# Another order of seven down-projection products, loads spread over items, and pinned weight sums in the up projection

## The chip, the cores and the metric

The kernel runs on one core of one Trainium2 chip. The metric is the device time of one execution in microseconds; the median over several runs is compared. A core has TensorE (PE) for matmuls, VectorE (DVE) and ScalarE (ACT) for elementwise work, GpSimd (POOL) and SyncE (SP), the last two here mostly issuing DMA transfers. Each engine works through its own queue in order; semaphores make one wait for another.

## The reference

One inference step of a two-layer encoder. There are 1024 frames of a prompt and 8 x 16 frames of running streams, T = 1152 tokens of width 1024. Layer 0 mixes with stick-breaking attention beside a convolution module, layer 1 with chunk-band attention; each layer ends with a squared-ReLU MLP of width 4096:

```python
def sq_relu_mlp(h, w_up, w_down):
    return jnp.square(jax.nn.relu(h @ w_up)) @ w_down

for layer in range(DEPTH):
    ...
    xp = xp + op
    xs = xs + os_
    xp = xp + sq_relu_mlp(rmsnorm(xp, norm_ffn[layer]), w_up[layer], w_down[layer])
    xs = xs + sq_relu_mlp(rmsnorm(xs, norm_ffn[layer]), w_up[layer], w_down[layer])
y_prompt = rmsnorm(xp, norm_final)
y_sample = rmsnorm(xs, norm_final)
```

All is float32. Beside y the step returns the new keys, values and convolution states. The change lies in the MLPs and at their borders.

## The kernel before, in words

**Data.** Activations lie feature by token, in tiles of 128 features by 1152 tokens. A product keeps float32 accuracy by splitting each operand into a high and a low part: ACT copies the high part (L180), DVE subtracts it to get the low part (L181), and each product is three matmuls (high by high and two mixed ones, `SPLIT`). One matmul has 288 token columns, a quarter of the tokens (TQ); TW = 576 is half of them.

**The MLP** of a layer is the function `rest`. It first finishes the out projection (evictions `evac`, L1303) and makes sums of activations (`combine`). Then both matrix products of the MLP are done by Strassen and Winograd's scheme, a 2x2 block product in seven products instead of eight.

*Up projection*: 16 units (`unit(m)`), each with products k = 0 to 6 of 24 matmuls. `seven(i)` makes the split weight of product i = 7m + k out of two raw tiles of `w_up` (`raw`, L1318 to L1323): for k = 1 the sums s1 = a21 + a22 (L1336), a21 - a11 (L1337) and s1 - a11 (L1338), the last being the weight of product 1; s1 itself is that of product 2; for k = 4 there is a difference at L1345. Split weights rotate through four tiles of a ring ("hl_m") and two others ("hl0", "hl1", printed as hl00 and hl10). The products go through three PSUM banks per token quarter. `take` evicts them: product 0 is copied by ACT (L1415), products 1 and 2 are added to the copy (L1417, L1419), and the quarters of the hidden block are finished at L1423 (product 4), L1426 (product 5) and L1429 (product 6). `done` then scales by the norm (L1394), applies relu and square on ACT (L1395, L1396), and makes three sums of the hidden blocks for the down projection, t3, t2 and b12 (L1400 to L1402); a fourth is `last_sum` (L1365). The seven combinations of hidden blocks go to DRAM (hb_d) through POOL's queue.

*Down projection*: seven products of 16 items each, 112 items, 24 matmuls per item (L1576). `todos` lists them in the order of `chains`; products of one chain accumulate in the same eight PSUM banks. Before, the chains are (3), (0, 1, 4), (2, 5), (6), and in layer 1 the last product is done one token quarter after another, with items of 12 matmuls. The loop at the end of `rest` does for each item i: load the hidden block and weight of item i + 4 (`load`), split those of i + 2 (`prep`: `split_b` for the hidden block, `split_w` for the weight), and the matmuls (`item`). At the last item of a product DVE adds the banks to the residual (L1582). Weight blocks a11, a21 and a22 are loaded once and stay (`resident`); products 3, 5 and 6 stream theirs. When a quarter of the output (a feature half by a token half) is final, `then` hands out the squares and splits of the next norm, done a step at a time among the later items. At item 104 of layer 0 `soon` loads and splits the first two weight chunks (each in two halves of 256 KB) of layer 1's first projection, through the staging tiles "st" that the streamed weights use.

**What sets the order.** The instructions are recorded in program order and then a list scheduler orders each engine's queue by its own estimates. `tc.keep_in_program_order` (`pinned`) keeps an instruction behind everything recorded before it on its engine. In the down projection nearly all of DVE's and ACT's work is pinned; in `seven` nothing is. DMA issues of loads stand in SP's queue in order.

Of the kernel before, what the change touches and what calls it, by code (L numbers as in the profile page):

```python
# [78 lines left out]
def level(steps, extra):  # L79


    pe, dve = sum(s.pe for s in steps), sum(s.dve for s in steps + extra)
    out, at, done, extra = [], 0.0, 0.0, list(extra)
    for s in steps:
        while extra and done + 0.5 * extra[0].dve < at / pe * dve:
            done += extra[0].dve
# [4 lines left out]
    return out + extra

# [27 lines left out]
def tile_trunk(ctx, tc, ins, outs):  # L120
# [1091 lines left out]
    def rest(layer, ks, cat, rst, mp, then, soon=None):  # L1212
# [112 lines left out]
        def seven(i):  # L1325
# [8 lines left out]
            elif k == 1:  # L1334
                s1 = ups["s1"] = sp.tile([P, 512], F32, "st", f"s1{name}{m}")
                tt(s1, a21, a22, ALU.add)  # L1336
# [16 lines left out]
            split(w[:, 0], w[:, 1], src)  # L1353
# [7 lines left out]
        pinned = tc.keep_in_program_order  # L1361
# [117 lines left out]
        def halves_of(t):  # L1479
            return [t[:, :512], t[:, 512:1024]]  # L1480

        def resident(kind, j):

            to = {"a11": a11, "a21": a21, "a22": a22}[kind]
            if j % 2 == 0:
                if kind == "a22":
                    tag = ("sl8", "sl9", "sl10", "sl11", "lo0", "lo1", "lo2", "xr3")[j // 2]
                    t = own(tag, F32)
                else:
                    t = place(j // 2, 0 if kind == "a11" else 1, F32, f"w{name}")  # L1490
                to[j], to[j + 1] = halves_of(t)
# [3 lines left out]
        def load(i):  # L1495

            if i >= len(todos):
                return
            k, ns, j = todos[i]
            if i == 0:  # L1500
# [6 lines left out]
            if k in (3, 5) or k == 6 and ns[0] == 0:  # L1507
                streams[i] = staging(wd[2 * j + 1][:, 512:] if k == 6 else wd[2 * j + 1][:, :512], f"wd{layer}{i}")
# [9 lines left out]
        def split_w(i):  # L1518
            k, ns, j = todos[i]
            if ns == (1,):  # L1520
                ws[i] = ws[i - 16]
                return
            if k == 3 or k == 6:
                src = streams.pop(i)
            elif k == 5:
                src = streams.pop(i)
                pinned(tt(src, src, a22[j], ALU.subtract))
# [6 lines left out]
            else:  # L1534
                src = a11[j] if k == 0 else a21[j]
            if k == 6 and layer == 1:
                w = pair(place(j // 2, j % 2, F32R, f"wk{name}"))
            elif k == 6:
                if j < 8:
                    tag = ("sl8", "sl9", "sl10", "sl11", "lo0", "lo1", "lo2", "xr3")[j]  # L1540
                    asplit.append(pair(own(tag, F32R)))
                w = asplit[j % 8]
# [7 lines left out]
        def prep(i):  # L1550
            if i < len(todos):
                split_b(i)
                split_w(i)

        def begin(n):

            if n == 0:
                for i in range(4):
                    load(i)
            else:  # L1560
                prep(0)
                prep(1)
# [3 lines left out]
        def item(i):  # L1566
            k, ns, j = todos[i]
            first = any(k == chain[0] for chain in chains) and j == 0
            b, w = bs.pop(i), ws[i]
            for m in range(4):  # L1570
                for n in ns:
                    if first:
                        banks[m, n] = bank(f"pd{layer}{k}{m}{n}")
                    ps = banks[m, n][:, :TQ]
                    for s, (a, h) in enumerate(SPLIT):
                        mm(ps, w[:, a, m * P:m * P + P], b[:, h, (n - ns[0]) * TQ:(n - ns[0]) * TQ + TQ],  # L1576
                           start=first and s == 0, stop=j == NF // 2 - 1 and s == 2,
                           skip_group_check=not any(k == chain[0] for chain in chains))
                    if j == NF // 2 - 1:
# [3 lines left out]
            if j == NF // 2 - 1 and k in final:  # L1583
# [11 lines left out]
        sq = Turns([extra[:, :TW], extra[:, TW:]])  # L1595
        for i in range(len(todos)):
            if i == 3:
                last_sum(NF // 2 - 1)
            if 2 <= i < 18:
                resident("a11", i - 2)  # L1600
            if 14 <= i < 30:
                resident("a21", i - 14)
            if 16 <= i < 32:
                resident("a22", i - 16)
            c = {n: m for m, n in enumerate((6, 7, 8, 9, 40, 41, 42, 43))}.get(i)
            if c is not None:
                x[c] = own(f"sl{c}", F32)
                dma(x[c], xr_d[layer][c])
            load(i + 4)
            prep(i + 2)  # L1610
            if 18 <= i < 34:
                pinned(tt(a21[i - 18], a21[i - 18], a11[i - 18], ALU.subtract))
# [6 lines left out]
        for go in later:  # L1619
# [219 lines left out]
```

## Time and profile before

| | us |
|---|---|
| runs | 2825.31, 2830.28, 2831.74 |
| median | 2830.28 |
| profiled execution | 2830.25 |
| its span | 2828.5 |
| out projection's end and unit 0, layer 0 (644 to 668) | 24.0 |
| up, layer 0 (668 to 1022.6) / layer 1 (2095 to 2447) | 354.6 / 352.0 |
| down, layer 0 (1022.6 to 1392) / layer 1 (2447 to 2816) | 369.4 / 369.0 |
| TensorE busy | 2705.3 |

A row of the timeline has the start in us, the time of the group, engine, line, operation, output tile <- input tiles, shape, the count, and in brackets the idle time before it and what ended it. A row of waits has who waited <- for whom, us in total, how many times, the longest. DVE at a line of the helper `split` has L181, ACT L180; the tile's name says which split it is.

### The profile page before, as it was taken

The page shows a single profiled execution, that of the slowest core. Times are in us where ns is not written, and L with a number is a line of the kernel's source. Part 1 is how long each engine was busy: PE and PEld are TensorE (multiplying, and loading weights), DVE is VectorE, ACT ScalarE, POOL GpSimd, SP SyncE. Part 2 cuts the span into 40 slices and gives each one's busy share as a digit, 9 for nine tenths or more (in the row PEclk, how much of TensorE's full clock was granted, in tenths as well). Part 3 has the DMA queues.
Part 4 walks back from the last instruction along what each step waited for, and adds up shares of the span by engine and source line. Part 5 has one row for each costly group of instructions (what it writes and reads, how often), then busy time and mean ns, then how long its engine had stood idle before and what let it go on. Part 6 is the DMA issues. An engine that isn't in the chain of part 4 may idle for free.

```text
span 2828.5 us, 50713 instructions
## 1 busy us (share of the span) xinstructions
PE 2705.3 (96%) x19362; PEld 2592.1 (92%) x19362; DVE 2146.1 (76%) x4201; ACT 1380.5 (49%) x2898; POOL 329.5 (12%) x599
## 2 busy tenths in 40 slices
PE   8988988899999999999999999998999999999998
PEld 8987876799999999999899999997999999999998
DVE  8999999978777756667467777778787777657676
ACT  5344446665444444445355555555554444434344
POOL 1000101032111110000011111110221111100001
PEclk9999998999999999999999999999999999999999
DMA  4434346443433486336444444446533334873355
GB/s 155 129 98 132 107 138 191 155 163 132 136 134 133 148 302 230 102 96 201 144 143 135 137 136 136 136 131 216 185 131 138 133 134 144 287 252 93 93 147 163
DMA packets 177811, 431.29 MB, mean 152 GB/s; under 512 B 26480, under 2 KB 54320, under 8 KB 175520
## 3 DMA queue, kind: packets, MB, share of 16 engines
q1 hardware_dynamic: 140304, 296.77, 33.6%
q0 software_dynamic: 37120, 131.27, 13.6%
q8 instruction: 152, 2.49, 0.4%
q14 instruction: 91, 0.75, 0.1%
q10 hardware_dynamic: 144, 0.02, 0.0%
HBM read 297.98 MB, written 117.34 MB: 147 GB/s over the span
## 4 chain that ended last, share of the span: by engine, by line
PE 51%; DVE 24%; DMA 10%; ACT 8%; issue 6%; SPq 0%; POOL 0%; DVEq 0%; ACTq 0%; POOLq 0%
PE pd L1576 19%; PE psc L220 10%; PE um L1388 9%; DMA xr<-in_w_up_dram 4%; DVE y L669 4%; DMA st_wd<-in_w_down_dram 3%; DVE kp L843 3%; PE avc L401 2%; DVE hl_m L181 2%; PE tpc L389 2%; DVE sg L845 1%; PE psoa L220 1%; PE f L220 1%; DMA wm<-in_w_down_dram 1%; DVE wla L181 1%
## 5 line engine op out<-in xcount | busy, mean ns | idle before, releaser
L220 PE MATMUL psc<-h,hl_wc 128*128 128x384 f32 x1728 | 327.2, 340 | 0.0
L220 PEld LDWEIGHTS psc<-h,hl_wc 128*128 128x128 f32 x1728 | 296.8, 188 | 13.3 <-issue 10.9
L1388 PE MATMUL um<-sl,hl_m 128*128 128x288 f32 x1548 | 244.1, 299 | 8.3 <-DVE hdm L1423 8.3
L1388 PEld LDWEIGHTS um<-sl,hl_m 128*128 128x128 f32 x1548 | 220.1, 191 | 10.7 <-ACT hdm L1396 5.8
L1576 PE MATMUL pd<-tm,hl_wd 128*128 128x288 f32 x1536 | 211.0, 296 | 2.1 <-DVE hl_wd L181 0.8
L1576 PEld LDWEIGHTS pd<-tm,hl_wd 128*128 128x128 f32 x1536 | 205.3, 189 | 4.5 <-DVE hl_wd L181 1.9
L669 DVE SCALAR_TENSOR_TENSOR y<-u,dw,y 128x1024 f32<-128x1024 f32 (+1 forms) x232 | 176.5, 809 | 0.4
L220 PE MATMUL psp<-h,hl_wi 128*128 128x384 f32 x864 | 169.0, 345 | 0.2 <-ACT kps L892 0.2
L1395 ACT ACTIVATE hdm<-hdm 128x288 f32<-128x288 f32 x192 | 84.4, 439 | 165.2 <-DVE hdm L1394 165.2
L220 PEld LDWEIGHTS psp<-h,hl_wi 128*128 128x128 f32 x864 | 149.7, 190 | 6.4 <-issue 4.9
L181 DVE TENSOR_TENSOR tm<-xr,tm 128x576 fp32r<-128x576 f32 (+1 forms) x120 | 85.7, 715 | 76.4 <-ACT tm L180 76.4
L180 ACT ACTIVATE tm<-xr 128x576 fp32r<-128x576 f32 (+1 forms) x120 | 77.8, 648 | 97.1 <-PE pd L1576 68.0
L1388 PE MATMUL um<-sl,hl 128*128 128x288 f32 x756 | 120.2, 297 | 4.4 <-DVE hdm L1423 4.4
L1104 ACT ACTIVATE s<-s,mxc 128x640 f32<-128x640 f32 (+4 forms) x128 | 88.8, 694 | 60.2 <-DVE mxc L1101 58.6
L180 ACT ACTIVATE hl_m<-xr 128x512 fp32r<-128x512 f32 x132 | 80.7, 621 | 71.8 <-DVE xr L1338 56.0
L1388 PEld LDWEIGHTS um<-sl,hl 128*128 128x128 f32 x756 | 106.5, 188 | 6.6 <-DVE hdm L1423 5.8
L1576 PE MATMUL pd<-th,hl_wd 128*128 128x288 f32 x768 | 108.3, 296 | 2.5 <-DVE th L181 2.3
L1576 PE MATMUL pd<-xr,hl_wd 128*128 128x288 f32 x768 | 108.1, 296 | 0.4 <-DVE hl_wd L181 0.4
L1576 PEld LDWEIGHTS pd<-th,hl_wd 128*128 128x128 f32 x768 | 103.7, 189 | 3.5 <-DVE th L181 3.0
L1576 PE MATMUL pd<-tm,hl 128*128 128x288 f32 x768 | 105.1, 295 | 0.0
L1576 PEld LDWEIGHTS pd<-xr,hl_wd 128*128 128x128 f32 x768 | 103.7, 189 | 1.2 <-DVE hl_wd L181 0.8
L181 DVE TENSOR_TENSOR hl_m<-xr,hl_m 128x512 fp32r<-128x512 f32 x132 | 92.3, 700 | 16.2 <-ACT hl_m L180 15.1
(527 smaller groups left out, 6814.4 us busy)
## 6 DMA issues: line engine op xcount, KB each, us to landing
xr<-hb_d SPq DMA_DIRECT2D x208, 288.0 KB, 2.9
xr<-in_w_up_dram SPq DMA_DIRECT2D x64, 512.0 KB, 4.8
hb_d<-hdm POOLq DMA_DIRECT2D x96, 288.0 KB, 3.7
hb_d<-t POOLq DMA_DIRECT2D x96, 288.0 KB, 3.7
st_wd<-in_w_down_dram SPq DMA_DIRECT2D x96, 256.0 KB, 3.4
wm<-in_w_down_dram SPq DMA_DIRECT2D x64, 256.0 KB, 6.0
st_wc<-in_w_in_c_dram SPq DMA_DIRECT2D x48, 256.0 KB, 2.8
xm_d<-xo POOLq DMA_DIRECT2D x16, 576.0 KB, 3.5
```

The costliest lines, as they stand in the source:

```text
L180: ACT(hi, src, AF.Copy)
L181: return tt(lo, src, f(hi), ALU.subtract)
L220: mm(ps()[:, :G], hl[:, a, at:at + P], act[g][k // 4][b][:, k % 4, :], start=n == 0, stop=n == len(todo) - 1)
L389: nc.tensor.transpose(tp[:, c0 + q * P:c0 + (q + 1) * P], blocks.get(j, tile_q), ident)
L401: mm(st["av"][:, o0:o0 + n], vs[:, j, i].rearrange("p a d -> p (a d)"), src[:, c0:c0 + n], start=st["done"] == 0, stop=st["done"] == nmm - 1)
L669: stt(src if j == CW - 1 else dst, src, wj, dst, ALU.mult, ALU.add)
L843: nc.vector.tensor_tensor_scan(keep[:, 0:n][:, ::-1], keep[:, 0:n][:, ::-1], ones[:, 0:1].to_broadcast([P, n]), 1.0, ALU.mult, ALU.mult)
L845: tt(w[:, 0:n - 1], w[:, 0:n - 1], keep[:, 1:n], ALU.mult)
L1104: ACT(s[:, :n], s[:, :n], AF.Exp, bias=mx, scale=-1.0, accum_out=tot)
L1388: mm(banks[b, n][:, :TQ], w[:, a, c * P:c * P + P], combo(key, c)[:, h, n * TQ:n * TQ + TQ], start=k < 3 and c == 0 and i == 0, stop=c == ...
L1395: ACT(y, y, AF.Relu)
L1576: mm(ps, w[:, a, m * P:m * P + P], b[:, h, (n - ns[0]) * TQ:(n - ns[0]) * TQ + TQ], start=first and s == 0, stop=j == NF // 2 - 1 and s == ...
```

## The change

1. *Up projection.* The sum s1 is pinned. So are the splits of product 0's weight, from unit 1 on. s1 of unit m + 1 is recorded in unit m just before product 6, behind the eviction of product 5 with its sums L1400 to L1402.

2. *Down projection.* The chains are (6), (3), (0, 1, 4), (2, 5), in layer 1 (6), (3), (0, 1, 4), (2), (5), where product 2 adds to two output quarters and product 5 goes quarter by quarter. The first half of the tokens is final after product 4, the fifth of seven, where before its last part came with the seventh product. Product 6 uses the resident a22, so 32 streamed 256-KB loads fall away. Item 0 opens all eight banks at once. Loads and splits are listed per item in a table `ahead_of`: a11 at items 8 to 23, a21 at 28 to 43, the residual at 2, 4, 6, 8 and 24 to 27; in layer 1 half of the last product's weights are split during product 2.

3. *First loads of layer 1.* `soon` now returns twelve steps, done at items 100 to 111 of layer 0: each of the four loads goes into half of the tile t1 and is split two items later.

4. At the borders the token order is mirrored: layer 1's first projections take token thirds 0, 1, 2 instead of 2, 0, 1, and the output's tail is the last 288 tokens instead of the second quarter.

The core of the diff:

```diff
+        pinned = tc.keep_in_program_order
...
                 s1 = ups["s1"] = sp.tile([P, 512], F32, "st", f"s1{name}{m}")
-                tt(s1, a21, a22, ALU.add)
+                pinned(tt(s1, a21, a22, ALU.add))
                 tt(a21, a21, a11, ALU.subtract)
                 tt(a11, s1, a11, ALU.subtract)
...
-            split(w[:, 0], w[:, 1], src)
+            if k == 0 and m:
+                pinned(ACT(w[:, 0], src, AF.Copy))
+                pinned(tt(w[:, 1], src, f(w[:, 0]), ALU.subtract))
+            else:
+                split(w[:, 0], w[:, 1], src)
...
-        chains = ((3,), (0, 1, 4), (2, 5), (6,))
-        out = {3: [(0, 0)], 0: [(0, 0)], 1: [(0, 1)], 4: [(1, 0), (1, 1)], 2: [(1, 1)], 5: [(0, 1)], 6: [(1, 0)]}
-        final = {0: (0, 0), 2: (1, 1), 5: (0, 1), 6: (1, 0)}
+        chains = ((6,), (3,), (0, 1, 4), (2, 5))
+        out = {6: [(1, 0)], 3: [(0, 0)], 0: [(0, 0)], 1: [(0, 1)], 4: [(1, 0), (1, 1)], 2: [(1, 1)], 5: [(0, 1)]}
+        final = {0: (0, 0), 4: (1, 0), 2: (1, 1), 5: (0, 1)}
...
+            chains = (*chains[:-1], (2,), (5,))
+            out[2].append((0, 1))
+            todos[6 * NJ:] = [(5, (n,), j) for n in range(2) for j in range(NJ)]
...
+        for i, (k, ns, j) in enumerate(todos):
+            at(max(-2, i - 4), load_b, i)
+            when = i - 2
+            if layer == 1 and k == 5:
+                when = 5 * NJ + 2 * j if j < 8 else i - 1 - (NJ - 1 - j)
+            at(max(-2, when - 2), load_w, i)
+            at(max(-1, i - 2), split_b, i)
+            at(max(-1, when), split_w, i)
...
+        for n, go in enumerate(soon(extra[:, TW:TW + 512]) if soon else []):
+            at(100 + n, go)
...
-            if i == 104 and soon:
-                soon()
```

Three places show how instructions move. The first is DVE in layer 0's up projection. The names: um0610 is the bank of layer 0, unit 6, bank 1, quarter 0; s1m06 the sum s1 of unit 6; hl_m043 the weight of its product 1 (43 = 7 x 6 + 1). Before, s1m06 stands among the evictions of unit 4:

```order
L1338 TENSOR_TENSOR xr20_6077<-s1m05_7990,xr20_6077 128x512
L1419 TENSOR_TENSOR tm00_6082<-um0420_7853,tm00_6082 128x288
L1336 TENSOR_TENSOR s1m06_8237<-xr10_6076 128x512
L1337 TENSOR_TENSOR xr10_6076<-xr10_6076,xr00_6075 128x512
L1419 TENSOR_TENSOR tm10_6083<-um0421_7867,tm00_6082 128x288
L181 TENSOR_TENSOR hl_m036_7994<-xr20_6077,hl_m036_7994 128x512
L1394 TENSOR_TENSOR th0_6723<-um0400_7788,rm0_6818 128x288
L1394 TENSOR_TENSOR th0_6723<-um0401_7802,rm0_6818 128x288
L181 TENSOR_TENSOR hl_m037_8032<-s1m05_7990,hl_m037_8032 128x512
L1423 TENSOR_TENSOR hdm0_51_6724<-um0410_7821,tm00_6082 128x288
```

In the changed kernel (line numbers are 5 to 9 higher: L1409 to L1411 are L1400 to L1402, L1438 is L1429, L1403 is L1394) the end of unit 5 and the making of unit 6's weights read so:

```order
L1409 TENSOR_TENSOR t10_6087<-hdm0_60_6725,hdm0_61_6726 128x576
L1403 TENSOR_TENSOR hdm0_61_6726<-hdm0_61_6726,rm0_6818 128x288
L1410 TENSOR_TENSOR t10_6087<-hdm0_60_6725,t10_6087 128x576
L1411 TENSOR_TENSOR hdm0_60_6725<-hdm0_60_6725 128x576
L1342 TENSOR_TENSOR s1m06_8237<-xr10_6076 128x512
L1438 TENSOR_TENSOR hdm0_61_6726<-um0511_8082,tm00_6082 128x288
L1343 TENSOR_TENSOR xr10_6076<-xr10_6076,xr00_6075 128x512
L1403 TENSOR_TENSOR hdm0_61_6726<-hdm0_61_6726,rm0_6818 128x288
L1344 TENSOR_TENSOR xr00_6075<-s1m06_8237,xr00_6075 128x512
L186 TENSOR_TENSOR hl00_6079<-xr10_6076,hl00_6079 128x512
L186 TENSOR_TENSOR hl_m043_8241<-xr00_6075,hl_m043_8241 128x512
```

So s1 has moved from two units ahead to the very end of the unit before, and the weight of product 1 (from xr00, made by L1344) follows seven rows behind the last sum, after the low half of product 4's weight (hl00).

The second is PE in unit 7 of layer 0, where product 0 (weight hl_m049) ends. Before, product 1 (hl_m050, operand t2) follows at once:

```order
L1388 MATMUL um0701_8543<-b11m0_30_6711,hl_m049_8443 128x288 x3
L1388 MATMUL um0710_8561<-t2m0_01_6289,hl_m050_8488 128x288 x3
L1388 MATMUL um0710_8561<-t2m0_11_6446,hl_m050_8488 128x288 x3
L1388 MATMUL um0710_8561<-t2m0_21_6593,hl_m050_8488 128x288 x3
L1388 MATMUL um0710_8561<-t2m0_31_6750,hl_m050_8488 128x288 x3
L1388 MATMUL um0711_8575<-t2m0_01_6289,hl_m050_8488 128x288 x3
```

In the changed kernel product 3 (hl00, operand b21) comes between, and product 1 starts inside its second quarter:

```order
L1397 MATMUL um0701_8543<-b11m0_30_6711,hl_m049_8443 128x288 x3
L1397 MATMUL um0700_8529<-sl20_6094,hl00_6079 128x288 x3
L1397 MATMUL um0700_8529<-sl30_6095,hl00_6079 128x288 x3
L1397 MATMUL um0700_8529<-lo10_6085,hl00_6079 128x288 x3
L1397 MATMUL um0700_8529<-b21m0_41_6780,hl00_6079 128x288 x3
L1397 MATMUL um0701_8543<-sl20_6094,hl00_6079 128x288
L1397 MATMUL um0710_8561<-t2m0_01_6289,hl_m050_8488 128x288 x2
L1397 MATMUL um0711_8575<-t2m0_01_6289,hl_m050_8488 128x288 x2
L1397 MATMUL um0701_8543<-sl20_6094,hl00_6079 128x288 x2
L1397 MATMUL um0720_8592<-sl00_6092,hl_m051_8526 128x288
```

Units 7, 8, 9 and their like are rearranged in this way; in units 5, 6, 11 and 12 product 1 still follows product 0 directly.

The third is SP's queue near the end of layer 0's down projection, the transfers of layer 1's first weights (in_w_in_c). Before, the four follow each other between two streamed weights:

```order
L187 DMA st_wd0107_14214<-in_w_down_dram 128x512
L1506 DMA xr00_10662<-hb_d0_116 128x576
L187 DMA st_wd0108_14245<-in_w_down_dram 128x512
L1506 DMA xr10_10663<-hb_d0_116 128x576
L187 DMA st_wc0_0_14275<-in_w_in_c_dram 128x512
L187 DMA st_wc0_1_14280<-in_w_in_c_dram 128x512
L187 DMA st_wc1_0_14285<-in_w_in_c_dram 128x512
L187 DMA st_wc1_1_14290<-in_w_in_c_dram 128x512
L187 DMA st_wd0109_14296<-in_w_down_dram 128x512
```

In the changed kernel they go to the tile t1 (t10), one at a time between other loads:

```order
L1724 DMA t10_6087<-in_w_in_c_dram 128x512
L192 DMA st_wd0106_14121<-in_w_down_dram 128x512
L1512 DMA xr00_10662<-hb_d0_116 128x576
L1724 DMA t10_6087<-in_w_in_c_dram 128x512
L192 DMA st_wd0107_14160<-in_w_down_dram 128x512
L1512 DMA xr00_10662<-hb_d0_116 128x576
L192 DMA st_wd0108_14197<-in_w_down_dram 128x512
L1512 DMA xr10_10663<-hb_d0_116 128x576
L1724 DMA t10_6087<-in_w_in_c_dram 128x512
L192 DMA st_wd0109_14233<-in_w_down_dram 128x512
L1512 DMA xr10_10663<-hb_d0_116 128x576
```

The four are spread over the last twelve items, and no staging tile is shared any more.

More of the change, by code (lines that the diff above doesn't have):

```diff
@@ L91, in level, with run_all @@
     return out + extra
+def run_all(gos):
+    for go in gos:
+        go()
 def run(steps):
@@ L318, in chunk_steps, with chunks_steps @@
         return steps
-    def chunks_steps(ns, got, ahead, h, ks, evac, name, depth=1, gs=range(NG)):
+    def chunks_steps(ns, got, ahead, h, ks, evac, name, depth=1):
         steps = [Step(0.0, lambda: [ahead(n) for n in range(ns[0], ns[-1] + depth + 1)])]
-        for g in gs:
+        for g in range(NG):
             for n in ns:
@@ L1485, in resident, with load_b @@
             if j % 2 == 0:
[L1486 to L1491, printed above, removed]
+                t = own(tags[j // 2], F32) if kind == "a22" else place(j // 2, int(kind == "a21"), F32, f"w{name}")
+                to[j], to[j + 1] = t[:, :512], t[:, 512:1024]
             row = 2 * j + (kind == "a22")
             dma(to[j], wd[row][:, :512] if kind == "a11" else wd[row][:, 512:])
-        def load(i):
-            if i >= len(todos):
-                return
+        def load_b(i):
             k, ns, j = todos[i]
-            if i == 0:
+            if not braw:
                 for n in range(2):
@@ L1534, in split_w @@
             else:
[L1535 to L1542, printed above, removed]
+                src = {6: a22, 0: a11, 4: a21}[k][j]
+            if k == 5 and layer == 1:
+                w = pair(place(j % 8, int(j < 8), F32R, f"wk{name}"))
+            elif k == 5 and j > 3:
+                if len(asplit) < 4:
+                    asplit.append(pair(own(tags[len(asplit)], F32R)))
+                w = asplit[j % 4]
             elif i % 6 < 4:
@@ L1548, in split_w, with at, residual @@
             ws[i] = w
[L1550 to L1553, printed above, removed]
-        def begin(n):
[L1557 to L1562, printed above, removed]
+        ahead_of = {i: [] for i in range(-2, len(todos))}
+        def at(i, go, *args):
+            ahead_of[i].append(lambda: go(*args))
+        for i, (k, ns, j) in enumerate(todos):
[6 more added lines that the diff above has]
+            at(max(-1, when), split_w, i)
+        for c, i in zip((4, 5, 6, 7, 0, 1, 2, 3), (2, 4, 6, 8, 24, 25, 26, 27)):
+            def residual(c=c):
+                x[c] = own(f"sl{c}", F32)
+                dma(x[c], xr_d[layer][c])
+            at(i, residual)
+        for j in range(NJ):
+            at(8 + j, resident, "a11", j)
+            at(28 + j, resident, "a21", j)
+            at(34 + j, lambda j=j: pinned(tt(a21[j], a21[j], a11[j], ALU.subtract)))
+        at(3, last_sum, NF // 2 - 1)
+        for n, go in enumerate(soon(extra[:, TW:TW + 512]) if soon else []):
+            at(100 + n, go)
+        def begin(n):
+            run_all(ahead_of.pop(n - 2))
         banks = {}
@@ L1567, in item @@
             k, ns, j = todos[i]
-            first = any(k == chain[0] for chain in chains) and j == 0
+            first = k in heads and j == 0
+            if first and k == 6:
+                banks.update({at: bank(f"pd{layer}{k}{at[0]}{at[1]}")
+                              for at in ((0, 0), (0, 1), (1, 0), (1, 1), (3, 0), (3, 1), (2, 0), (2, 1))})
             b, w = bs.pop(i), ws[i]
@@ L1571, in item @@
                 for n in ns:
-                    if first:
+                    if first and k != 6:
                         banks[m, n] = bank(f"pd{layer}{k}{m}{n}")
@@ L1576, in item @@
                         mm(ps, w[:, a, m * P:m * P + P], b[:, h, (n - ns[0]) * TQ:(n - ns[0]) * TQ + TQ],
-                           start=first and s == 0, stop=j == NF // 2 - 1 and s == 2,
-                           skip_group_check=not any(k == chain[0] for chain in chains))
-                    if j == NF // 2 - 1:
+                           start=first and s == 0, stop=j == NJ - 1 and s == 2, skip_group_check=k not in heads)
+                    if j == NJ - 1:
                         for e, half in out[k]:
@@ L1594, in rest @@
             unit(m)
-        sq = Turns([extra[:, :TW], extra[:, TW:]])
+        sq = Turns([extra[:, :TW]] if soon else [extra[:, :TW], extra[:, TW:]])
         for i in range(len(todos)):
[L1597 to L1612, printed above, removed]
+            run_all(ahead_of[i])
             item(i)
-            if i == 104 and soon:
-                soon()
             for _ in range(1 + (len(later) > len(todos) - i)):
```

104 lines of the change are left out of this document (56 added, 48 removed).

## The prediction, on record before the run

> **What bounds the kernel now.** I read the page first, then busy time by stage, then TensorE's waits in the stages that the change touches, and last the rows around each wait.
>
> ```profile
> span 2828.5 us, 50713 instructions
> PE 2705.3 (96%) x19362; PEld 2592.1 (92%) x19362; DVE 2146.1 (76%) x4201; ACT 1380.5 (49%) x2898; POOL 329.5 (12%) x599
> 668.00:1022.60 354.60, 347.02 (x2592) 344.32 (x2591) 260.94 (x507) 174.12 (x395) 57.77 (x107) 1.00 0.43 149
> 1022.60:1392.00 369.40, 361.49 (x2693) 359.30 (x2691) 235.83 (x383) 155.69 (x253) 10.25 (x19) 0.99 0.56 175
> 2095.00:2447.00 352.00, 346.94 (x2595) 344.80 (x2594) 261.64 (x508) 174.34 (x396) 58.26 (x108) 1.00 0.43 150
> 2447.00:2816.00 369.00, 363.71 (x2712) 359.16 (x2711) 239.55 (x425) 151.79 (x265) 10.83 (x21) 1.00 0.53 166
> ```
>
> The columns of the last four rows are length, then busy time of PE, weight loads, DVE, ACT and POOL, granted clock, DMA share and GB/s. The rows are the up projections (units 1 to 15) and the down projections, layer 0 and layer 1. TensorE does the same matmuls before and after, so only its idle time and its clock can change: some 5 to 8 us in each up and down stage. Of the up stages the waits of PE and of DVE say this (us in total, times, longest), layer 0 first:
>
> ```profile
> PE um L1388 <- DVE hdm L1423: 7.6, 10, 1.3
> DVE s1m L1336 <- DMA xr<-in_w_up_dram: 40.0, 13, 4.2
> PE um L1388 <- DVE hdm L1423: 5.1, 8, 0.9
> DVE s1m L1336 <- DMA xr<-in_w_up_dram: 37.2, 13, 3.6
> ```
>
> One unit shows how they hang together:
>
> ```profile
> 805.96 0.69 DVE L1336 TENSOR_TENSOR s1m<-xr 128x512 f32<-128x512 f32 x1 [3.33 <-DMA xr<-in_w_up_dram]
> 806.68 0.69 DVE L1337 TENSOR_TENSOR xr<-xr,xr 128x512 f32<-128x512 f32 x1
> 807.29 0.45 DVE L1419 TENSOR_TENSOR tm<-um,tm 128x288 f32<-128x288 f32 x1
> 810.83 0.45 DVE L1423 TENSOR_TENSOR hdm<-um,tm 128x288 f32<-128x288 f32 x1
> 811.42 1.43 PE L1388 MATMUL um<-sl,hl_m 128*128 128x288 f32 x9 [0.57 <-DVE hdm L1423]
> ```
>
> The scheduler put the weight sum s1 of a unit two units ahead into DVE's queue. It waits 3.33 us there for its load, the evictions behind it come late, and product 6, which needs the bank that L1423 reads, waits 0.57 us.
>
> The down projection's one large loss is at the end of layer 0:
>
> ```profile
> 1358.08 12.39 SPq L187 DMA_DIRECT2D st_wc<-in_w_in_c_dram x4
> 1361.20 3.36 PE L1576 MATMUL pd<-xr,sl 128*128 128x288 f32 x24
> 1364.40 4.42 PE L1576 MATMUL pd<-tm,sl 128*128 128x288 f32 x32
> 1374.65 4.33 PE L1576 MATMUL pd<-tm,sl 128*128 128x288 f32 x16 [5.82 <-DVE tm L181]
> 1378.78 3.75 PE L1576 MATMUL pd<-th,lo 128*128 128x288 f32 x24
> 1382.37 0.83 PE L1576 MATMUL pd<-xr,lo 128*128 128x288 f32 x5
> 1376.00:1378.00 2.00, 2.00 (x10) 2.00 (x9) 1.51 (x3) 0.63 (x1) 0.00 (x0) 0.50 0.90 300
> ```
>
> An item of 24 matmuls takes 3.20 us (1361.20 to 1364.40), 0.133 us each. Four 256-KB loads of the next projection's weights, issued over 12.39 us on SP's queue, and their splits stand ahead of the split that the next item needs.
>
> **The change, part by part.** All is set against the profiled execution, 2830.25 us, within 0.1 us of the median 2830.28.
>
> *The stall at the end of layer 0* goes: the loads are one at a time, three items apart, in a buffer that no item uses, and the splits two items behind them. It is worth 10.25 − 32 × 0.133 = 5.98 us (1364.40 to 1374.65), plus the half clock after it: 16 matmuls in 4.13 us rather than 2.13, and the next 24 in 3.59 rather than 3.20. **−8.4 us**, of which a clock drop by itself is 2.4.
>
> *The waits of the up projections* go with s1's early place: **−12.7 us** (7.6 + 5.1).
>
> *What the pin on s1 adds.* It puts s1 behind everything traced before, which is the end of the unit before. In the order of the changed kernel DVE does, around the start T0 of unit 6: L1409, L1403, L1410, L1411, then s1 (L1342), L1438, L1343, L1403, L1344, then a split of product 4, and only then the low half of product 1's weight, which L1344 makes. In the last unit of before DVE is on time and TensorE sets the pace, so the place of these instructions relative to a unit's end can be read there; 1022.71 is that end:
>
> ```profile
> 1021.68 0.75 DVE L1400 TENSOR_TENSOR t<-hdm,hdm 128x576 f32<-128x576 f32 x1
> 1022.35 0.45 DVE L1394 TENSOR_TENSOR hdm<-hdm,rm 128x288 f32<-128x288 f32 x1
> 1022.72 0.75 DVE L1401 TENSOR_TENSOR t<-hdm,t 128x576 f32<-128x576 f32 x1
> 1023.39 0.75 DVE L1402 TENSOR_TENSOR hdm<-hdm 128x576 f32<-128x576 f32 x1
> 1024.05 0.75 DVE L181 TENSOR_TENSOR th<-xr,th 128x576 fp32r<-128x576 f32 x1
> 1022.71 1.10 PE L1576 MATMUL pd<-th,hl_wd 128*128 128x288 f32 x7
> 1024.86 2.13 PE L1576 MATMUL pd<-th,hl_wd 128*128 128x288 f32 x14 [1.05 <-DVE th L181]
> 802.35 0.63 ACT L180 ACTIVATE hl_m<-xr 128x512 fp32r<-128x512 f32 x1 [2.36 <-DVE xr L1338]
> 798.56 0.40 ACT L1415 ACTIVATE tm<-um 128x288 f32<-128x288 f32 x1
> ```
>
> The instruction behind L1402 starts at T0 + 1.34; s1 takes that place. With steps of 0.61 for 128x512 (806.68 to 807.29) and 0.37 for 128x288 (1022.35 to 1022.72) follow L1438 at T0 + 1.95, L1343 at 2.32, L1403 at 2.93, L1344 at 3.30, done at 3.99. ACT's high half can start at 4.03, but ACT's queue has the high half of product 4, a relu and product 0's second copy (0.40 us) ahead of it: 4.4 to 5.05. TensorE wants it at T0 + 3.20, when product 0 ends, and gets it at about 5.1; the low half follows after the four matmuls that need only the high one and costs 0.1 to 0.2 more. So a unit of this kind waits **1.9 to 2.0 us**, once. TensorE's order has nothing else between product 0 and product 1 in units 5, 6, 11 and 12, 4 in each layer, 8 in all: 8 × 1.95 = 15.6. In units 4 and 10 a little of product 3 stands there, but the split waits behind other splits: 4 × 1.5 = 6. In the other 9 of each layer much of product 3 is moved ahead of product 1 and hides it but for about 0.23 us: 18 × 0.23 = 4.1. Together **+25.7 us**. By the dependence alone, without ACT's queue, it is 4.65 − 3.2 = 1.5, 1.0 and 0.1: 17.8. That is the lower end; the upper, with one more step of 0.61 ahead of the split in the twelve late units, is 33.
>
> *Unit 0* makes s1 behind the last evictions of the out projection. The stretch is DVE's already, 21.77 of 24 us:
>
> ```profile
> 644.00:668.00 24.00, 22.07 (x127) 20.89 (x126) 21.77 (x52) 12.36 (x23) 4.79 (x5) 0.79 0.42 136
> 644.63 2.56 PE L1388 MATMUL um<-b11m,hl_m 128*128 128x288 f32 x18
> 678.06 2.14 PE L1388 MATMUL um<-b11m,hl_m 128*128 128x288 f32 x15
> ```
>
> It takes 33.4 us instead of 22.4, at a clock of 0.79. DVE's work is the same, in another order, so I put **+2 us** on both layers (−2 to +8).
>
> *The down projections* are otherwise even. The 1.05 us at 1024.86 stay: the low split is again behind L1411, with the last eviction now ahead of it. The 32 loads that fall away were hidden. In layer 1 product 2 adds to two halves, 16 adds rather than 8 before the quarters of product 5, whose items last 1.6 us:
>
> ```profile
> L1582 DVE TENSOR_TENSOR sl<-sl,pd 128x288 f32<-128x288 f32 x63 | 24.7, 453 | 10.4 <-PE pd L1576 10.3
> 1287.00:1338.00 51.00, 51.00 (x386) 51.00 (x385) 38.52 (x61) 24.21 (x40) 2.16 (x4) 1.00 0.67 202
> ```
>
> Eight adds are 3.6 us of DVE at 0.45; splits are made two items ahead, so most is hidden: **+1.5** (0 to 3.6). In layer 0 product 5 is now last and its 16 subtractions meet the squares and splits of the next norm. DVE had 12.5 us free of 51 in that product; about twelve more steps of 128x576 at 0.75 (1022.72) are 9 us and fit: 0 (to +3).
>
> Sum: −8.4 − 12.7 + 25.7 + 2 + 1.5 = **+8.1**, 2838.4 us, if the clock holds.
>
> *The clock.* A pause of TensorE can halve its clock. The rows nearest to a 2.0 us pause:
>
> ```profile
> 223.55 0.66 PE L389 MATMUL tpa<-ident,sg 128*128 128x128 f32 x4 [1.96 <-DVE sg L845]
> 223.00:225.00 2.00, 1.45 (x11) 1.40 (x12) 2.00 (x3) 0.84 (x2) 0.47 (x1) 1.00 0.50 203
> 414.07 0.45 PE L516 MATMUL sn<-ident,sgs 128*128 128x128 f32 x1 [2.18 <-DVE sgs L845]
> 414.00:416.00 2.00, 1.93 (x8) 1.81 (x9) 2.00 (x3) 0.79 (x3) 0.00 (x0) 0.50 0.00 0
> ```
>
> After 1.96 us the clock stayed at 1.00, after 2.18 it was 0.50. The eight long pauses lie between, so 0 to 8 of them drop the clock, at 2.4 us each as at 1374.65: 0 to 19 us. They are nearer to the row that kept the clock; I take one: **2840.8 us**.
>
> [...]
>
> **The rivals.** *The pin is free* (the other side): product 1's weight is there when product 0 ends. The waits go, nothing comes: −8.4 − 12.7 + 2 + 1.5 = −17.6, 2812.7 us. It decides at T0 + 3.2: L1344 would have to end by T0 + 2.5, that is the sums t2 and b12 (L1400 to L1402) would have to run 1.5 us sooner than in the last unit of before. For it: DVE has no 3 to 4 us waits any more. Against: these sums follow TensorE's last two products through ACT, not DVE's load. Chance 0.15.
>
> *Only the dependence costs*: ACT's queue is not in the way, 17.8 instead of 25.7, and the time is 2830.4, no change. Against: product 0's copy cannot start before TensorE ends product 0. Chance 0.25, with smaller misses of the other terms (2820 to 2836).
>
> *No clock drop*: 2838.4, chance 0.22; *one to four drops*, 2840.8 to 2848, 0.25; *more, up to eight*, to 2857.6, 0.13.
>
> *The change of the first loads does not act*: SP issues the spread loads in its own order, and if one is still queued behind a wait, the 8.4 us stay and 2849 results; it is inside the range.
>
> **How the numbers follow.** The likeliest is the sum with one drop, 2841. The range reaches from 2820, below the case without change, to 2858, all eight drops; the free pin is left out. 0.2% is 5.7 us, about what a measurement of this kernel tells from no change: 2824.6 to 2835.9. Faster is the free pin, 0.15; same is the dependence alone, 0.25; slower is the three clock cases, 0.60.
>
> **What would show it.** Right: in the up stages no wait on L1432 (L1423 of before) and DVE's s1 with no DMA wait, but TensorE waiting 1.9 to 2.3 us for product 1's weight in units 5, 6, 11 and 12 of both layers, about 1.5 in 4 and 10, some 26 us in all; the wait of 5.8 us at the end of layer 0's down projection gone. Wrong: up stages shorter than 354.6 and 352.0 us, or s1 starting earlier than 1.3 us after a unit's end.

## The result, and the profile after

The changed kernel takes 2843.95 us (median of 4 runs, 2843.25 to 2845.48), the kernel before 2828.97 beside it (4 runs, 2825.31 to 2831.74). The ratio is 1.0054, 95% interval 1.0037 to 1.0072: slower by 15 us. The profiled execution spans 2843.7 us against 2828.5.

The page of the changed kernel, its head and the chain:

```profile
span 2843.7 us, 50617 instructions
PE 2708.6 (95%) x19362; PEld 2594.6 (91%) x19362; DVE 2151.5 (76%) x4209; ACT 1394.2 (49%) x2898; POOL 327.8 (12%) x599
PE 71%; DVE 17%; ACT 6%; issue 3%; DMA 2%; DVEq 0%; SPq 0%; ACTq 0%
```

TensorE's busy time is the same to 3.3 us, so 12 of the 15 us are idle time. To see where, I cut both traces at the same points of the program: the first matmul of unit 0, of unit 1 and of the down projection, in each layer, and the first matmul after it. The windows of the changed kernel (length first, then busy time of PE, weight loads, DVE, ACT and POOL, clock, DMA share, GB/s):

```profile
645.64:682.03 36.39, 29.34 (x193) 28.26 (x193) 27.04 (x64) 18.57 (x37) 4.14 (x6) 0.86 0.31 107
682.03:1028.47 346.44, 339.25 (x2522) 335.43 (x2521) 255.59 (x493) 171.73 (x376) 56.68 (x105) 1.00 0.42 148
1028.47:1392.34 363.87, 358.62 (x2691) 357.84 (x2689) 235.47 (x383) 156.78 (x256) 10.25 (x19) 1.00 0.53 165
1392.34:2068.92 676.58, 658.25 (x4642) 622.59 (x4641) 498.16 (x1328) 360.52 (x818) 98.01 (x195) 0.99 0.49 151
2068.92:2105.87 36.95, 28.95 (x193) 27.86 (x193) 27.94 (x65) 19.52 (x39) 5.10 (x7) 0.86 0.31 106
2105.87:2452.45 346.58, 339.40 (x2523) 335.56 (x2521) 255.59 (x493) 171.72 (x376) 56.69 (x105) 1.00 0.41 148
2452.45:2843.70 391.25, 369.56 (x2744) 365.03 (x2742) 247.89 (x448) 159.43 (x279) 11.30 (x21) 0.99 0.49 151
```

The same windows of the kernel before:

```profile
644.63:678.06 33.43, 31.50 (x193) 29.79 (x193) 29.85 (x70) 20.45 (x42) 5.41 (x6) 0.85 0.35 117
678.06:1022.71 344.65, 337.07 (x2522) 334.90 (x2521) 252.33 (x490) 166.03 (x376) 56.66 (x105) 1.00 0.44 152
1022.71:1391.97 369.26, 361.35 (x2691) 359.16 (x2690) 235.69 (x383) 155.66 (x253) 10.25 (x19) 0.99 0.56 175
2104.79:2446.51 341.72, 336.66 (x2522) 334.92 (x2521) 252.45 (x490) 166.06 (x376) 56.67 (x105) 1.00 0.44 153
2446.51:2828.50 381.99, 368.57 (x2744) 363.23 (x2742) 245.59 (x440) 157.42 (x276) 11.31 (x21) 0.99 0.53 163
```

| stage | before | after | difference |
|---|---|---|---|
| ahead of unit 0, layer 0 | 644.63 | 645.64 | +1.0 |
| unit 0, layers 0 and 1 | 33.43, 34.18 | 36.39, 36.95 | +5.7 |
| units 1 to 15, layers 0 and 1 | 344.65, 341.72 | 346.44, 346.58 | +6.7 |
| down, layer 0 | 369.26 | 363.87 | -5.4 |
| layer 1's mixer | 678.64 | 676.58 | -2.1 |
| down and tail, layer 1 | 381.99 | 391.25 | +9.3 |

The waits in the units: of the changed kernel TensorE's are, in either layer,

```profile
PE um L1397 <- ACT hl_m L185: 5.9, 4, 1.5
PE um L1397 <- ACT tm L1424: 1.2, 2, 0.6
```

The wait for the evictions of product 4 is gone. Four waits for product 1's weight (hl_m) have come, in units 5, 6, 11 and 12, and in units 4 and 10 two for the copy of product 0 (tm). One of the four, at the start of unit 6 of layer 0:

```profile
797.29 3.33 PE L1397 MATMUL um<-b11m,hl_m 128*128 128x288 f32 x24
798.64 0.68 DVE L1342 TENSOR_TENSOR s1m<-xr 128x512 f32<-128x512 f32 x1
800.58 0.68 DVE L1344 TENSOR_TENSOR xr<-s1m,xr 128x512 f32<-128x512 f32 x1
801.20 0.39 ACT L1424 ACTIVATE tm<-um 128x288 f32<-128x288 f32 x1
801.49 0.62 ACT L185 ACTIVATE hl_m<-xr 128x512 fp32r<-128x512 f32 x1
802.16 3.64 PE L1397 MATMUL um<-t2m,hl_m 128*128 128x288 f32 x24 [1.53 <-ACT hl_m L185]
```

With T0 = 797.29, s1 starts at T0 + 1.35, L1344 at 3.29, ACT's high half at 4.20 behind product 0's copy, and TensorE goes on at 4.87. The unit takes 24.3 us.

The stall of 5.8 us at the end of layer 0's down projection is gone, but item 0 of both down projections has a new one. Layer 0:

```profile
1028.47 1.09 PE L1607 MATMUL pd<-th,hl_wd 128*128 128x288 f32 x7
1032.93 0.40 PE L1607 MATMUL pd<-th,hl_wd 128*128 128x288 f32 x1 [3.37 <-DVE hdm L1438]
1034.94 3.67 PE L1607 MATMUL pd<-th,hl_wd 128*128 128x288 f32 x16 [1.60 <-DVE th L186]
1031.75 0.76 DVE L1409 TENSOR_TENSOR t<-hdm,hdm 128x576 f32<-128x576 f32 x1 [3.73 <-ACT hdm L1405]
1024.27 0.63 ACT L185 ACTIVATE hl_wd<-lo 128x512 fp32r<-128x512 f32 x1 [3.78 <-DMA lo<-in_w_down_dram]
1029.91 0.63 ACT L185 ACTIVATE hl<-lo 128x512 fp32r<-128x512 f32 x1 [1.53 <-DMA lo<-in_w_down_dram]
```

The rows are read from the bottom. ACT waits 3.78 and 1.53 us for the first resident blocks of a22, which land in tiles lo that the up projection used. Behind that wait are the last relu and square of unit 15 (L1405); DVE waits 3.73 us for them at L1409; the eviction that frees the eighth bank is next in DVE's queue; and TensorE waits 3.37 us for that bank. From item 0's first matmul to item 4's it is 19.49 us instead of 14.81 in layer 0, and 20.65 instead of 15.28 in layer 1: 10.1 us together.

### The profile page after: what moved, and what is told of

It reads as the page before. It is cut to its first block, busy times and chain, and to the rows that moved or that the text cites. A ratio compares the mean times of both kernels' runs of the same rounds, so it can differ in the third digit from the quotient of the medians.

```text
span 2843.7 us, 50617 instructions
## 1 busy us (share of the span) xinstructions
PE 2708.6 (95%) x19362; PEld 2594.6 (91%) x19362; DVE 2151.5 (76%) x4209; ACT 1394.2 (49%) x2898; POOL 327.8 (12%) x599
## 4 chain that ended last, share of the span: by engine, by line
PE 71%; DVE 17%; ACT 6%; issue 3%; DMA 2%; DVEq 0%; SPq 0%; ACTq 0%
PE um L1397 24%; PE pd L1607 23%; PE psc L225 10%; DVE y L674 4%; DVE kp L848 3%; PE avc L406 2%; PE tpc L394 2%; DVE sg L850 1%; PE psoa L225 1%; PE f L225 1%; DVE wla L186 1%; PE zc L1142 1%; PE psob L225 1%; PE zc L1143 1%; PE psp L225 1%
## 5 line engine op out<-in xcount | busy, mean ns | idle before, releaser
L1607 PEld LDWEIGHTS pd<-tm,hl_wd 128*128 128x128 f32 x1584 | 211.3, 189 | 2.1 <-ACT hl_wd L185 2.1
L1607 PE MATMUL pd<-th,hl_wd 128*128 128x288 f32 x792 | 115.5, 300 | 9.8 <-DVE hdm L1438 6.6
L1607 PEld LDWEIGHTS pd<-th,hl_wd 128*128 128x128 f32 x792 | 110.2, 193 | 10.7 <-DVE hdm L1438 7.0
L1397 PE MATMUL um<-t2m,hl_m 128*128 128x288 f32 x528 | 84.3, 311 | 26.9 <-ACT hl_m L185 26.9
L1607 PEld LDWEIGHTS pd<-tm,hl 128*128 128x128 f32 x768 | 103.2, 188 | 2.1 <-ACT hl L185 2.0
```

The costliest lines, as they stand in the source:

```text
L1397: mm(banks[b, n][:, :TQ], w[:, a, c * P:c * P + P], combo(key, c)[:, h, n * TQ:n * TQ + TQ], start=k < 3 and c == 0 and i == 0, stop=c == ...
```

## The experiments

Times of kernels of different runs are compared by their ratio to the kernel before on the same chip, and by the stages of their profiled executions. The time ahead of unit 0 varied from 644.6 to 649.6 us among kernels that have the same work there, so differences of a few us are read from the stages.

**The pins alone.** The kernel before with

```diff
-                tt(s1, a21, a22, ALU.add)
+                pinned(tt(s1, a21, a22, ALU.add))
...
+            if k == 0 and m:
+                pinned(ACT(w[:, 0], src, AF.Copy))
+                pinned(tt(w[:, 1], src, f(w[:, 0]), ALU.subtract))
```

> The kernel before with the two pins of the up projection (s1, and the split of product 0's weight) and nothing else. Theory A (the pin of s1 makes product 1's weight late): units 1 to 15 take 346.4 and 346.6 us as in the changed kernel instead of 344.7 and 341.7, unit 0 takes 36.4 and 36.9 instead of 33.4 and 34.2, all else as before: 2829 + 12.4 = 2841 us. Theory B (the pins are harmless or good, the loss sits in the new down projection): the up waits of 12.7 us go, 2816 to 2829 us.

Measured: 2836.94 us, ratio 1.0046 (1.0031 to 1.0061). Units 1 to 15 take 346.5 and 346.9 us, unit 0 35.7 and 37.1. The slower up projections come from the pins alone, and all units of these but one take the same time as in the changed kernel to 0.1 us (24.18 and 24.26 for units 5 and 6).

**s1 unpinned in the changed kernel.**

```diff
-                pinned(tt(s1, a21, a22, ALU.add))
+                tt(s1, a21, a22, ALU.add)
```

> The changed kernel with s1 unpinned; the split of product 0's weight stays pinned. Theory A: no wait of TensorE for product 1's weight any more, the waits for the evictions of product 4 come back, up projections and unit 0 about as in the kernel before: 2844 - 12.4 = 2831.6 us, between 2828 and 2835. Rival (the pinned split of product 0's weight is what holds up product 1): the waits of 1.8 us in units 5, 6, 11 and 12 stay, 2840 to 2846 us.

Measured: 2812.19 us, ratio 0.9952 (0.9934 to 0.9969). The waits for product 1's weight are gone, so it was s1's pin. But the old waits did not come back either, against both theories: units 1 to 15 take 334.65 us in both layers, with TensorE busy for every one of them:

```profile
676.03:1010.68 334.65, 334.65 (x2523) 334.65 (x2522) 249.26 (x489) 167.45 (x374) 56.81 (x105) 1.00 0.44 156
DVE s1m L1342 <- DMA xr<-in_w_up_dram: 28.4, 13, 4.5
```

And s1 still waits for its load there, 28.4 us in all in layer 0. The prediction's cause of the old waits (s1 blocks DVE's queue) is not sufficient.

**Only the other pin.** The kernel before with the split of product 0's weight pinned and nothing else:

```diff
+            if k == 0 and m:
+                pinned(ACT(w[:, 0], src, AF.Copy))
+                pinned(tt(w[:, 1], src, f(w[:, 0]), ALU.subtract))
+            else:
+                split(w[:, 0], w[:, 1], src)
```

> The kernel before with the split of product 0's weight pinned and nothing else. If that pin alone cures the up projections: units 1 to 15 at 334.7 us in both layers (344.7 and 341.7 before), unit 0 30.3 and 31.3 (33.4 and 34.2), the stall at the end of layer 0 still there: 2829 - 10 - 7 - 6 = 2806 us, ratio about 0.992. If s1's wait for its load is what makes the evictions late, as the prediction had it: 2825 to 2829, ratio 1.

Measured: 2806.19 us, ratio 0.9934 (0.991 to 0.9959). Units 1 to 15 take 334.65 and 334.64 us, unit 0 29.9 and 31.0. Over units 1 to 15 of layer 0, s1 still waits for its load, once for 3.8 us, which is longer than in the unit that the prediction showed. DVE's waits for ACT's high halves of the ring's weights have nearly gone (first row the kernel before, then this one):

```profile
DVE hl_m L181 <- ACT hl_m L180: 16.7, 27, 1.1
DVE s1m L1337 <- DMA xr<-in_w_up_dram: 29.4, 13, 3.8
DVE hl_m L181 <- ACT hl_m L180: 3.6, 4, 1.1
```

So one of the two pins takes out all of the old waits and the other brings the new ones. s1m06 stands at the same row of DVE's queue as before. What differs is what stands between it and the first eviction of product 4 behind it. Before, that is L1337, L1419, two scaling steps and two low halves of unit 5's weights (hl_m036, hl_m037, in the first rows of the section on the change). With product 0's split pinned the two low halves stand behind the evictions. In the trace of before the second of them waited another 1.14 us for ACT in the unit that the prediction showed:

```profile
810.22 0.69 DVE L181 TENSOR_TENSOR hl_m<-s1m,hl_m 128x512 fp32r<-128x512 f32 x1 [1.14 <-ACT hl_m L180]
810.83 0.45 DVE L1423 TENSOR_TENSOR hdm<-um,tm 128x288 f32<-128x288 f32 x1
```

That these steps behind the load, and not the load's wait by itself, make the eviction late follows from the order. It was not tried apart, and s1's wait is shorter too (29.4 us in all, 40.0 before), so that may have a part in it.

**Neither pin in the changed kernel.**

```diff
-                pinned(tt(s1, a21, a22, ALU.add))
+                tt(s1, a21, a22, ALU.add)
...
-            if k == 0 and m:
-                pinned(ACT(w[:, 0], src, AF.Copy))
-                pinned(tt(w[:, 1], src, f(w[:, 0]), ALU.subtract))
-            else:
-                split(w[:, 0], w[:, 1], src)
+            split(w[:, 0], w[:, 1], src)
```

> The changed kernel without either pin: only the down projections, the spread loads and the borders are new. Up projections as in the kernel before (344.7 and 341.7 for units 1 to 15, 33 for unit 0). What the rest of the change is worth, from the stages of the changed kernel: -5.4 and -2.1 in layer 0 and layer 1's mixer, +9.3 in layer 1's down projection, about 2829 + 2 = 2831 us, ratio 1.000 to 1.001. If the pin of product 0's split is not what cured the up projections, these are 334.7 here too and the time is 2812.

Measured: 2831.0 us, ratio 1.0016 (1.0002 to 1.0031); units 1 to 15 at 345.3 and 342.4, unit 0 at 30.3 and 31.6. The rest of the change, without the pins, costs some 4.5 us (0.16% of 2825), at the edge of what the runs can tell.

**s1 one product sooner.** In the changed kernel s1 and its two differences are pinned right behind product 0's split, and s1 of unit 0 is not pinned:

```diff
+        def sums(m, keep):
+            ...
+            keep(tt(s1, a21, a22, ALU.add))
+            keep(tt(a21, a21, a11, ALU.subtract))
+            keep(tt(a11, s1, a11, ALU.subtract))
...
+            if k == 0 and m:
+                sums(m, pinned)
```

> The changed kernel with s1 and the two differences that follow it pinned one product sooner, right behind the split of product 0's weight (ahead of product 5's eviction instead of behind it); in unit 0 s1 is not pinned. Theory A: product 1's weight is ready before product 0 ends, and DVE waits for no load: units 1 to 15 take 22.3 to 22.4 us each, 335 to 336 a layer instead of 346.5, unit 0 33.4 and 34.2: 2844 - 22 - 5.7 = 2816 us, between 2812 and 2822. Rival (DVE has too much to do in a unit, so something is late wherever s1 stands): waits of TensorE of over 5 us a layer move to the evictions, and the time is over 2828 us.

Measured: 2814.4 us, ratio 0.9969 (0.9957 to 0.9982), units 1 to 15 at 334.64 and 334.65. DVE has time enough; it is the place of s1, one product (3.2 us) too late, that cost.

**The spread loads alone.** The kernel before with `soon` as twelve steps at items 100 to 111.

```diff
-        rest(0, range(3, KC), cat, rst, mp, then0, lambda: (win[1](0), win[1](1)))
+        rest(0, range(3, KC), cat, rst, mp, then0, soon)
...
-            if i == 104 and soon:
-                soon()
+            if i in steps:
+                steps[i]()
```

> The kernel before with the first four 256-KB loads of layer 1's projection spread over items 100 to 111 through one half of the tile t1 (the squares of the norm in layer 0 get one buffer instead of two, as in the changed kernel). Theory A: the wait of 5.8 us and the half clock behind it go, nothing else moves: 2829 - 8.4 = 2820.6 us, between 2818 and 2823. Rival (the loads are held up in SP's queue wherever they are issued): the wait shrinks only in part and another item waits, 2824 to 2830 us.

Measured: 2819.08 us, ratio 0.998 (0.997 to 0.999). Layer 0's down projection takes 359.77 us instead of 369.26, 9.5 less. The runs show less: by the ratio it is some 5.6 us, between 2.8 and 8.5. The changed kernel took 363.87, 4.1 more, which is about what item 0's new waits cost it (19.49 - 14.81 = 4.7).

**The streamed product first.** The changed kernel with the chains (3), (6), (0, 1, 4), (2, 5), and with item 0 opening its banks one by one, as in the kernel before:

```diff
-        chains = ((6,), (3,), (0, 1, 4), (2, 5))
+        chains = ((3,), (6,), (0, 1, 4), (2, 5))
...
-        for c, i in zip((4, 5, 6, 7, 0, 1, 2, 3), (2, 4, 6, 8, 24, 25, 26, 27)):
+        for c, i in zip((0, 1, 2, 3, 4, 5, 6, 7), (2, 4, 6, 8, 24, 25, 26, 27)):
...
-            if first and k == 6:
-
-                banks.update({at: bank(f"pd{layer}{k}{at[0]}{at[1]}")
-                              for at in ((0, 0), (0, 1), (1, 0), (1, 1), (3, 0), (3, 1), (2, 0), (2, 1))})
...
-                    if first and k != 6:
+                    if first:
```

> The changed kernel, both pins kept, with the down projections' chains in the order (3), (6), (0, 1, 4), (2, 5): the first product streams its weights as in the kernel before, and a22 is needed only from item 16 on. Theory C (item 0 waits because a22's first loads come late and hold up ACT, and with it the unit's last evictions): the waits of 3.4 and 1.6 us in item 0, in both layers, shrink to about 1 us and the half clock behind them goes: -4 us in layer 0, -6 in layer 1, 2844 - 10 = 2834 us. Rival (opening eight banks at once causes it, or the saturated DMA queues hold up whatever comes first): the waits stay, 2840 to 2845 us.

Measured: 2836.36 us, ratio 1.0039 (1.0025 to 1.0053), an interval that overlaps that of the changed kernel, so the gain is read from the stages. Layer 0's down projection takes 359.0 us (363.87 with product 6 first), layer 1's with the tail 385.69 (391.25): -4.9 and -5.6, as expected. Item 0 reads as before the change again:

```profile
1027.41 1.10 PE L1603 MATMUL pd<-th,hl_wd 128*128 128x288 f32 x7
1029.56 2.12 PE L1603 MATMUL pd<-th,hl_wd 128*128 128x288 f32 x14 [1.05 <-DVE th L186]
```

This edit takes out a22's early loads and the opening of all eight banks together, so by itself it does not say which of the two cost the time. Kernels that keep the opening say more. With s1 unpinned, layer 1's item 0 has these rows:

```profile
2420.65 0.64 ACT L185 ACTIVATE hl<-lo 128x512 fp32r<-128x512 f32 x1 [0.51 <-DMA lo<-in_w_down_dram]
2423.68 0.40 PE L1607 MATMUL pd<-th,hl_wd 128*128 128x288 f32 x1 [0.82 <-DVE hdm L1438]
```

Where ACT's later wait for a22 is 0.51 us instead of 1.46, TensorE's wait for the bank is 0.82 instead of 3.19. So most of the wait for the bank comes from the loads. The second pause stays at 1.60 us there, and item 0 to item 4 still take 17.20 us, where the kernel before takes 15.28; what causes this rest was not tried.

**Product 2's sum an item earlier.** In the changed kernel:

```diff
             elif k == 2:
-                pinned(tt(a11[j], a11[j], a22[j], ALU.add))
                 src = a11[j]
...
+            if k == 2:
+                at(i - 3, lambda j=j: pinned(tt(a11[j], a11[j], a22[j], ALU.add)))
```

> The changed kernel, both pins kept, with product 2's weight sum (a11 + a22 on DVE) done one item earlier than the split that needs it. Theory D (in layer 1 DVE and ACT wait for each other three times per two items of product 2, sum, copy, low half, which makes the pair take 7.45 us instead of 6.4): the five waits of 0.7 to 0.84 us there go, layer 1's last part shortens by 4 to 5 us, 2839.5 us. Rival (DVE or ACT has simply too much to do there): the waits stay or move, over 2842 us.

The changed kernel's waits in this product, in layer 1, and one of them with DVE's rows:

```profile
PE pd L1607 <- ACT hl_wd L185: 2.5, 3, 0.8
PE pd L1607 <- ACT hl L185: 1.8, 3, 0.8
2752.18 0.68 DVE L1543 TENSOR_TENSOR wm<-wm,sl 128x512 f32<-128x512 f32 x1
2753.55 0.69 DVE L186 TENSOR_TENSOR hl_wd<-wm,hl_wd 128x512 fp32r<-128x512 f32 x1 [0.69 <-ACT hl_wd L185]
2753.58 3.44 PE L1607 MATMUL pd<-tm,hl_wd 128*128 128x288 f32 x24 [0.84 <-ACT hl_wd L185]
```

DVE makes the sum (L1543), waits 0.69 us for ACT to copy it, and makes the low half. Measured with the sum ahead: 2836.96 us, ratio 1.0046 (1.0031 to 1.0061), whose interval overlaps that of the changed kernel. In the profiled execution TensorE's two waits above are gone, and layer 1's last part takes 380.14 us instead of 391.25. From item 4's first matmul to the last product's it is 292.8 us instead of 299.4; another 2.4 are at item 0, where the wait for the bank was 1.96 instead of 3.19, and 2.0 in the tail. The first of these, 6.7, is the experiment's (4 to 5 were expected); the others I can't put down to it.

**All three in the new order.** s1 unpinned, product 3 first, product 2's sum earlier.

> The changed kernel with s1 unpinned (the split of product 0's weight pinned), the chains in the order (3), (6), (0, 1, 4), (2, 5), and product 2's sum an item earlier. If theories A, C and D hold and add up: 2812 - 10 - 4.5 = 2798 us, between 2793 and 2803. If C and D are wrong: 2810 to 2814.

Measured: 2796.37 us, ratio 0.9903 (0.9888 to 0.9918), where 2798 was expected. The three add up. **And the old order with the two edits that help:** the kernel before, product 0's split pinned, the loads spread.

> The kernel before, in its old order of products, with the split of product 0's weight pinned (s1 not) and the four loads spread. If the pin of product 0's split alone cures the up projections: units 1 to 15 take 334.7 us in each layer, unit 0 30.4 and 31.4, layer 0's down projection 360: 2829 - 10 - 7 - 6 - 9 = 2797 us, so that the new order of the products brings nothing by itself. If it needs the new order too: 2815 to 2820 us.

Measured: 2795.7 us, ratio 0.9898 (0.9883 to 0.9913). Both versions are 1% below the kernel before, and they can't be told apart: the new order of the products by itself brings nothing that can be measured.

## Why the prediction was right, point by point

The forecast was slower, 2841 us, and 2843.95 was measured. The sign and its main cause held: without s1's pin the changed kernel is faster (ratio 0.9952). That the total came so near is luck in part. Two parts of it, the units and the down projections, missed in opposite directions, and one part of the reasoning was wrong.

- **Product 1's weight late because of s1's pin**: right, by the pins alone and by s1 unpinned. The walk through the queues was exact to 0.01 us on DVE (s1 at T0 + 1.35 for 1.34, L1344 at 3.29 for 3.30); TensorE went on at 4.87, where 5.1 was forecast, since ACT had less ahead of the split. Against units of 22.31 the loss is 346.44 - 334.65 = 11.8 and 346.58 - 334.65 = 11.9, 23.7 in all, for 25.7 forecast. Set against the same units with s1 unpinned, units 4 and 10 lost 1.4 and units 5, 6, 11 and 12 between 1.8 and 2.0, as expected. The other nine of a layer lost 0.1 to 0.2 each, less than the 0.23 forecast, and this is most of the difference of 2.0.
- **The old waits go, -12.7**: they went, but were worth 344.65 - 334.65 = 10.0 and 341.72 - 334.65 = 7.1, 17.1 in all. The sum of named waits leaves out what the matmuls behind a wait lose: TensorE's busy time was 337.07 in the window where it is 334.65 without waits. And the cause was mistaken: the pin that took them out was that of product 0's split, for which the prediction has no term.
- **Unit 0, +2**: +5.7, inside the bounds of -2 to +8. TensorE has one new long wait there, 8.0 us in layer 1 and this one in layer 0:

```profile
656.04 1.33 PE L1397 MATMUL um<-t2m,hl_m 128*128 128x288 f32 x4 [7.05 <-ACT hl_m L185]
```

Unit 0 also varies by itself: in the profiled executions without s1's pin it took 29.9 to 33.4 us in layer 0, the longest at a clock of 0.85.

- **The stall at the end of layer 0, -8.4**: -9.5 in the profiled stage when it is done alone, about 5.6 by the runs (2.8 to 8.5).
- **The down projections otherwise even, "the 1.05 us at 1024.86 stay"**: this failed. The prediction looked at DVE's order there and not at ACT's, where the splits of a22 wait for loads ahead of the unit's last relu. It cost 10.1 us in both layers together. The step "item 0 opens all eight banks at once" was named in the change and given no price either; the eighth bank is what TensorE waited for, and the experiments do not part this step fully from the loads.
- **The boundary in layer 1, +1.5**: the adds there cost a wait of 0.73 us. What costs more is the product ahead of it, whose items wait for the weights as DVE and ACT take turns: from item 4 to the last product's start 299.4 us instead of 295.9.
- **One clock drop in the units**: none. The pauses were 1.44 and 1.53 us, not 2.0, and the clock in units 1 to 15 was 1.00 throughout. The drops came in item 0 instead, after 3.19 and 1.60 us of pause with one matmul between:

```profile
2456.73 0.40 PE L1607 MATMUL pd<-th,hl_wd 128*128 128x288 f32 x1 [3.19 <-DVE hdm L1438]
2458.73 4.21 PE L1607 MATMUL pd<-th,hl_wd 128*128 128x288 f32 x16 [1.60 <-DVE th L186]
2458.00:2463.00 5.00, 4.27 (x18) 4.27 (x19) 5.00 (x10) 0.47 (x2) 0.71 (x2) 0.50 1.02 349
```

In the windows' sum, 6.7 + 5.7 - 5.4 + 9.3 - 2.1 + 1.0 = 15.2 stands against 8.1 + 2.4 = 10.5. The units were 6.3 us better than forecast (+6.7 for 25.7 - 12.7 = +13.0), the down projections 10.8 worse (+3.9 for -8.4 + 1.5 = -6.9), and unit 0 3.7 worse. With the measured 17.1 and 23.7 in place of 12.7 and 25.7 the prediction's own sum would have been +1.7, or +4.1 with its clock drop, which is no change by its limit of 5.7 us. The losses in item 0 and in product 2, which it had put at little or nothing, made up for it.

## What to carry to other kernels

A pin does not put an instruction where it is needed but behind everything recorded ahead of it, so ask first what the last of these is and when it runs; here the same pin, recorded one product sooner, cost nothing. When a scheduler's order is at fault, change one pin at a time: of two pins in one edit one was worth -17 us in the units and the other +24. When a first load is moved, read the queue of the engine that consumes it as well as the one that computes, since that engine's older work, the last steps of the stage before, can stand behind the wait, as unit 15's last relu stood behind ACT's 3.78 us for a22.

## What the runs showed of the hardware

Pauses of 1.44 and 1.53 us did not drop TensorE's clock in the eight units that had them: it was 1.00 over units 1 to 15 of both layers. In item 0 of the changed kernel the clock fell behind two pauses with a single matmul between, to 0.57 behind 3.37 and 1.60 us in layer 0 (1034 to 1038) and to 0.50 behind 3.19 and 1.60 us in layer 1. Where the two were 1.96 and 1.60 us (product 2's sum an item earlier, layer 1) it was 0.56 just behind them:

```profile
2457.93 0.40 PE L1608 MATMUL pd<-th,hl_wd 128*128 128x288 f32 x1 [1.96 <-DVE hdm L1438]
2459.93 3.78 PE L1608 MATMUL pd<-th,hl_wd 128*128 128x288 f32 x16 [1.60 <-DVE th L186]
2460.00:2463.50 3.50, 3.50 (x16) 3.50 (x17) 3.50 (x7) 0.44 (x1) 0.54 (x1) 0.56 0.98 352
```

The 16 matmuls took 3.78 us there. Behind pauses of 1.45 and 1.60 us 16 matmuls took 2.40 us (neither pin, layer 0).

A limit for the length of a single pause, as the prediction sought it between 1.96 and 2.18 us, does not fit the rows. The pause of 1.96 us that kept the clock in the trace of before (1.00 also from 225.40 to 228.80) stands in the changed kernel's trace too, and there the clock fell to 0.50 behind it. The changed kernel's row, the 3.41 us ahead of its drop and the 3.41 us after, and last the 3.41 us ahead of the drop in layer 1's item 0:

```profile
223.88 0.66 PE L394 MATMUL tpa<-ident,sg 128*128 128x128 f32 x4 [1.96 <-DVE sg L850]
222.03:225.44 3.41, 1.56 (x12) 1.52 (x13) 3.41 (x6) 0.96 (x2) 0.55 (x1) 1.00 0.33 132
225.44:228.85 3.41, 3.41 (x17) 2.17 (x16) 3.30 (x7) 0.02 (x1) 2.68 (x5) 0.50 0.73 217
2454.35:2457.76 3.41, 0.40 (x1) 0.19 (x1) 2.21 (x4) 3.41 (x8) 0.67 (x2) 1.00 1.05 415
```

In the traces of before and after the stretches at half clock, the last of each trace aside, lasted 3.41 us nine times, 6.83 us twelve times and 10.24 us six times. In the 3.41 us ahead of the two drops above TensorE was busy for 1.56 and 0.40 us. In unit 0 of the kernel before the clock fell to 0.50 at 656.04 though TensorE counts as busy for 3.08 of the 3.41 us ahead of it, in part with matmuls of a single column. What sets off a drop is not shown by these runs.
